# Rotary key on 128 partitions, the shifts' second half by way of DRAM, rotated queries scaled in PSUM, maxima 0.3 steps earlier

## The chip, the cores and the metric

One Trainium2 chip, one core. The metric is the device time of one execution in microseconds (us); the kernel before takes 1496.21 us, the median of 3 runs. Engines are named as in the profile: PE is TensorE (matmul), PEld its weight loads, DVE is VectorE, ACT is ScalarE, POOL is GpSimd, and SP is the queue that issues all of this kernel's DMAs. L550 is line 550 of the kernel before.

## The reference

One layer of an encoder on x of 1024 tokens by 1024 columns, all in f32. Behind the norm and one projection `h @ w_in`, two groups of eight heads attend side by side, then come an output projection and a feed-forward block with a convolution of width 3. The change touches the two groups:

```python
# group A: softmax over three dilated windows, mixed by their denominators
for window, dilation in ((128, 1), (512, 4), (2048, 16)):
    o, lse = _dilated_branch(q, k, v, slopes, window, dilation)
# group B: latent attention with one rotated key for all heads
q = (_rmsnorm(c_q, q_lat_norm) @ w_uq).reshape(b, s, N_HEADS_B, QK_NOPE + QK_ROPE)
q_rope = _rope(q[..., QK_NOPE:], cos[:, None, :], sin[:, None, :])
k_rope = _rope(k_r, cos, sin)
sc = (q_nope @ k_nope + q_rope @ k_rope) * scale
```

`_rope` turns the two halves of 32 rows: `[x1*cos - x2*sin, x2*cos + x1*sin]`.

## The kernel before

Matmuls run in pieces of a high and a low part (three matmuls for each product, L95 to L97), so TensorE has most of the work. The program is a list of events, each a function with a due time in steps (`at`, `spread`). `run` goes through it by these times; an event that is not on the main line is put behind the last main event that is `LAG` steps older. A scheduler then orders the instructions of each engine, and each engine takes them in that order, without overtaking. One step is a chunk of scores; a head of group A has eight, so head h begins at step T = 8 h.

Head h of group A needs a row of shifts before its scores: the negative maxima of its scores, so that the exponentials stay small. `a_max` spreads eight steps of maxima over T + 1.1 to T + 5.8 of the head before: L534 multiplies, L537 on VectorE adds the table and takes a maximum for each of 128 rows into `m`, 16 columns: eight for blocks in natural order, eight for blocks in the order of residues by 4. Then `a_shift` (L542) transposes `m` to 16x128 (L545), negates it on ACT into `mt`, and two DMAs (L548, L549) lay it out as two rows of 1024 on partition 96 of the head's tile, where 64 other rows are the queries and keys. One VectorE instruction on one partition, L550, reads the second row in permuted order and writes the smaller of both to partition 64. The matmuls with 65 rows (L571, L607) take this row, so the first of them waits for L550; L570 and L606, with 128 rows, don't.

Group B starts from latents: five tiles of 128 rows kept in DRAM (`latd`). `latent_pool` loads the table of cosines and sines (`rope`, 128x2x1024) and the raw rotary key to partitions 64 to 128 of `kr`. `rope_key` (L783 to L785) turns the key with three VectorE instructions on 32 partitions of 1024 elements. `key_rows` puts the result as high and low part (L791 on ACT, L792 on VectorE) into rows 64 to 96 of one head tile, and a DMA (L794) copies them to the other. `scale_queries` loads the row of the queries' norm, `rq`, to all partitions and multiplies both halves of `rope` by it on GpSimd (L756), so that `rope_steps` (L879 to L881, twice for each of two groups of four heads) only multiplies the projection by the table. For the other queries L919 scales the projection in PSUM.

The maxima of group B (L944 matmul, L945 row maximum, L950 the larger of two halves, L952 the transposition) and its V projections (`bv_steps`, into `VH` and `VL` by L212) begin while head 7 of group A still runs. L968 is its first score. `pbank` gives out the PSUM banks, `eng` the engine from the table `ENG`.

## Time and profile before

| | us |
|---|---|
| median of 3 runs (1493.6 to 1498.79) | 1496.21 |
| the profiled execution | 1493.47 |
| its span | 1491.6 |
| PE busy | 1406.6 (94%) |
| DVE busy | 975.0 (65%) |
| ACT busy | 705.4 (47%) |
| POOL busy | 532.5 (36%) |

The mean granted clock of TensorE is 0.975. All times in the rows are from the start of this one execution's span, which takes 1.9 us less than the execution itself and 4.6 us less than the median. Group A's heads run until about 435 us, group B's until about 705; the output projection and the feed-forward block come behind. The shares over the whole span say little on a stage: in 40 slices PE has nine tenths or more nearly everywhere, and 7 in two slices between 335 and 410 us.

### The profile page before, as it was taken

The page shows a single profiled execution, that of the slowest core. Times are in us where ns is not written, and L with a number is a line of the kernel's source. Part 1 is how long each engine was busy: PE and PEld are TensorE (multiplying, and loading weights), DVE is VectorE, ACT ScalarE, POOL GpSimd, SP SyncE. Part 2 cuts the span into 40 slices and gives each one's busy share as a digit, 9 for nine tenths or more (in the row PEclk, how much of TensorE's full clock was granted, in tenths as well). Part 3 has the DMA queues.
Part 4 walks back from the last instruction along what each step waited for, and adds up shares of the span by engine and source line. Part 5 has one row for each costly group of instructions (what it writes and reads, how often), then busy time and mean ns, then how long its engine had stood idle before and what let it go on. Part 6 is the DMA issues. An engine that isn't in the chain of part 4 may idle for free.

```text
span 1491.6 us, 18735 instructions
## 1 busy us (share of the span) xinstructions
PE 1406.6 (94%) x6481; PEld 1117.6 (75%) x6481; DVE 975.0 (65%) x1637; ACT 705.4 (47%) x1274; POOL 532.5 (36%) x443
## 2 busy tenths in 40 slices
PE   7999999997899999899988699999999999999998
PEld 6788887876676677566666478888888887788886
DVE  6465453438876766443588778766666675884687
ACT  6244343325455556644644454444444444454444
POOL 3132222215444543322425355555555552000110
PEclk9999999997999999999999799999999999999999
DMA  5522343556434222630125023333333323864435
GB/s 189 122 70 64 79 102 87 171 136 188 95 72 105 61 44 66 163 75 25 60 96 179 26 80 118 107 107 106 100 100 104 107 92 120 288 213 150 120 98 198
DMA packets 135903, 167.06 MB, mean 112 GB/s; under 512 B 17443, under 2 KB 93616, under 8 KB 134144
## 3 DMA queue, kind: packets, MB, share of 16 engines
q1 hardware_dynamic: 135808, 165.87, 37.8%
q8 instruction: 51, 0.84, 0.2%
q14 instruction: 44, 0.36, 0.1%
HBM read 106.12 MB, written 39.43 MB: 98 GB/s over the span
## 4 chain that ended last, share of the span: by engine, by line
PE 53%; DVE 6%; ACT 3%; POOL 3%; issue 2%; DMA 1%; SPq 0%; DVEq 0%; POOLq 0%; ACTq 0%
PE u_pu L1268 4%; PE u_pu L1266 4%; PE u_pu L1267 4%; PE v_pu1v L1266 3%; PE v_pu1v L1268 3%; PE v_pu1v L1267 3%; PE X_acc L1507 2%; PE X_acc L1508 2%; PE X_acc L1506 2%; PE Y_acc L1508 2%; PE Y_acc L1507 2%; PE Y_acc L1506 2%; PE g_pu1g L1267 2%; PE g_pu1g L1268 2%; PE g_pu1g L1266 2%
## 5 line engine op out<-in xcount | busy, mean ns | idle before, releaser
L348 POOL TENSOR_TENSOR pl_pA<-sx_pA,ph_pA 128x512 fp32r<-128x512 f32 (+1 forms) x125 | 162.7, 1307 | 263.1 <-ACT sx_pA L92 129.8
L1246 POOL TENSOR_TENSOR w_pF<-S_pF,w_pF 128x512 fp32r<-128x512 f32 x88 | 128.6, 1463 | 108.1 <-ACT w_pF L92 77.5
L1246 POOL TENSOR_TENSOR w_pF<-wf_pF,w_pF 128x512 fp32r<-128x512 f32 x66 | 89.2, 1352 | 95.7 <-ACT w_pF L92 95.3
L95 PE MATMUL proj_psx<-hT_hT,wh_pA 128*128 128x512 f32 (+2 forms) x304 | 119.6, 393 | 0.0
L97 PE MATMUL proj_psx<-hT_hT,wl_pA 128*128 128x512 f32 (+2 forms) x304 | 118.4, 389 | 0.0
L96 PE MATMUL proj_psx<-hT_hT,wh_pA 128*128 128x512 f32 (+2 forms) x304 | 118.2, 389 | 0.1
L945 DVE TENSOR_REDUCE m_pA<-mx_psy 128x1 f32<-128x512 f32 x126 | 84.1, 687 | 33.6 <-PE mx_psy L944 32.6
L92 ACT ACTIVATE w_pF<-S_pF 128x512 fp32r<-128x512 f32 x88 | 55.1, 628 | 78.6 <-PE u_pu L1268 40.1
L92 ACT ACTIVATE w_pF<-ar_pD 128x512 fp32r<-128x512 f32 x77 | 48.6, 631 | 92.4 <-PE Y_acc L1508 43.7
L92 ACT ACTIVATE sx_pA<-s_ps 128x512 f32<-128x512 f32 x128 | 75.1, 597 | 30.7 <-PE s_ps L970 17.4
L1266 PE MATMUL u_pu<-T_h2T,w_pF 128*128 128x512 f32 x220 | 86.4, 394 | 1.5 <-ACT c_h2T L92 1.5
L1267 PE MATMUL u_pu<-T_h2T,w_pF 128*128 128x512 f32 x220 | 86.4, 393 | 0.0
L1268 PE MATMUL u_pu<-T_h2T,w_pF 128*128 128x512 f32 x220 | 86.2, 392 | 0.1
L1468 DVE TENSOR_TENSOR w_pF<-ar_pD,w_pF 128x512 fp32r<-128x512 f32 x77 | 55.6, 722 | 46.8 <-ACT w_pF L92 46.7
L337 DVE TENSOR_TENSOR sx_pA<-s_ps,tab_pA 128x256 f32<-128x256 f32 (+1 forms) x128 | 48.3, 410 | 53.4 <-PE s_ps L607 34.1
L537 DVE CUSTOM_DVE_ANT_0 mx_psx<-mx_psx,tab_pA 128x256 f32<-128x256 f32 (+1 forms) x112 | 47.2, 421 | 47.9 <-PE mx_psx L534 44.5
L229 POOL TENSOR_TENSOR wl_pA<-wf_pA,wh_pA 128x256 fp32r<-128x256 f32 x48 | 37.4, 805 | 112.8 <-ACT wh_pA L92 100.1
L92 ACT ACTIVATE ph_pA<-s_ps 128x512 fp32r<-128x512 f32 x85 | 50.5, 597 | 46.7 <-PE s_ps L970 46.3
L1507 PE MATMUL X_acc<-w_pF,w_pF 128*128 128x512 f32 x176 | 68.9, 391 | 2.3 <-DVE w_pF L1470 2.3
L1506 PE MATMUL X_acc<-w_pF,w_pF 128*128 128x512 f32 x176 | 68.5, 389 | 0.0
L1508 PE MATMUL X_acc<-w_pF,w_pF 128*128 128x512 f32 x176 | 68.5, 389 | 0.0
L97 PEld LDWEIGHTS proj_psx<-hT_hT,wl_pA 128*128 128x128 f32 (+1 forms) x304 | 57.4, 189 | 12.7 <-issue 0.4
(453 smaller groups left out, 4125.9 us busy)
## 6 DMA issues: line engine op xcount, KB each, us to landing
wf_pF<-in_w_up SPq DMA_DIRECT2D x44, 512.0 KB
ar_pD<-aD_dr SPq DMA_DIRECT2D x77, 256.0 KB
head_pA<-x_xr SPq DMA_DIRECT2D x22, 512.0 KB
aD_dr<-vt_aT SPq DMA_DIRECT2D x44, 256.0 KB
B_pD<-in_w_down SPq DMA_DIRECT2D x44, 256.0 KB
aD_dr<-gt_aT SPq DMA_DIRECT2D x33, 256.0 KB
wf_pA<-in_w_in SPq DMA_DIRECT2D x16, 512.0 KB
head_pA<-x_xr SPq DMA_DIRECT2D x24, 256.0 KB
```

The source lines that it names most:

```text
L92: nc.scalar.activation(o, i, func, **kw)
L95: i = mm(ps, ah, bh, start=first, stop=False)
L96: mm(ps, ah, bl, start=False, stop=False)
L97: mm(ps, al, bh, start=False, stop=last)
L348: e.tensor_tensor(pl[:, cs], pf[:, cs], f32(ph[:, cs]), op=ALU.subtract)
L1246: nc.gpsimd.tensor_tensor(w[:, 1], src, f32(w[:, 0]), op=ALU.subtract)
L1266: mm(bank, w[:, 0, k], m[:, 0, k], start=first, stop=False, skip_group_check=True)
L1267: mm(bank, w[:, 0, k], m[:, 1, k], start=False, stop=False, skip_group_check=True)
L1268: mm(bank, w[:, 1, k], m[:, 0, k], start=False, stop=last, skip_group_check=True)
L1506: mm(bank, wa[:, 0, ts], wb[:, 0], start=first, stop=False, skip_group_check=True)
L1507: mm(bank, wa[:, 0, ts], wb[:, 1], start=False, stop=False, skip_group_check=True)
L1508: mm(bank, wa[:, 1, ts], wb[:, 0], start=False, stop=last, skip_group_check=True)
```

## The change

The shift (`a_shift`): the first eight columns go to partitions 96 to 104 of the head's tile, eight rows of 128. The other eight go to a small DRAM array `shiftd` and come back from there in permuted order, 1024 runs of one element, onto the same eight partitions. The min is then an 8x128 instruction, and a fourth DMA lays its result out as the row on partition 64. The rotary key: `kr` is now 128 partitions by four blocks of 256, loaded by four DMAs (both halves of the key, cosine, sine), turned by three VectorE instructions and split by ACT and a fourth; two DMAs store high and low part in DRAM (`krd`), and each head tile gets its rows by two loads from there. The rotated queries: L756 is gone, and the projection is scaled in PSUM by a new VectorE instruction ahead of L879. The maxima of heads 1 to 6 are due from T + 0.8 to T + 5.2.

```diff
-                a_max(h + 1, T + 1.1, T + 5.8)
+                a_max(h + 1, T + 0.8, T + 5.2)
...
-        nc.sync.dma_start(f32(ht[96:97, 2, :]), mt[0:8, :])
-        nc.sync.dma_start(f32(ht[96:97, 3, :]), mt[8:16, :])
-        eng("min", 0).tensor_tensor(ht[64:65, 2, :].rearrange("p (i r) -> p i r", r=4),
-                                f32(ht[96:97, 2, :]).rearrange("p (i r) -> p i r", r=4),
-                                f32(ht[96:97, 3, :]).rearrange("p (r i) -> p i r", r=4), op=ALU.min)
+        d = shiftd[h % 2]
+        m = ht[96:104, 2:4, :P]
+        nc.sync.dma_start(f32(m[:, 0]), mt[0:8, :])
+        nc.sync.dma_start(d, mt[8:16, :])
+        nc.sync.dma_start(f32(m[:, 1]).rearrange("i (q r) -> i q r", r=4), d.rearrange("(r j) (b q) -> (j b) q r", j=2, b=4))
+        eng("min", 0).tensor_tensor(m[:, 0], f32(m[:, 0]), f32(m[:, 1]), op=ALU.min)
+        nc.sync.dma_start(f32(ht[64:65, 2, :]), f32(m[:, 0]))
...
         nc.sync.dma_start(L["rq"], rowd[1].partition_broadcast(P))
-        for i in range(2):
-            t = L["rope"][:, i, :]
-            eng("rope", i).tensor_tensor(t, t, L["rq"], op=ALU.mult)
...
-        L["kr"] = L["p"].t([P, S], "kr")
+        L["kr"] = L["p"].t([P, 4, 256], "kr", F32R)
...
-        nc.sync.dma_start(L["kr"][64:128], latd[2, :64])
+        for i, part in enumerate((latd[2, :32], latd[2, 32:64], rope[0, 64:96], rope[1, 96:128])):
+            nc.sync.dma_start(f32(L["kr"][:, i]), part.rearrange("d (a b) -> (d a) b", a=4))
...
-        t = pa.t([P, S], "tmp", bufs=2)[0:32]
-        eng("kr", 0).tensor_tensor(t, kr[96:128], rp[96:128, 1, :], op=ALU.mult)
-        eng("kr", 1).tensor_tensor(kr[0:32], kr[64:96], rp[64:96, 0, :], op=ALU.mult)
-        eng("kr", 2).tensor_tensor(kr[0:32], kr[0:32], t, op=ALU.subtract)
+        for i in range(2):
+            nc.vector.tensor_tensor(kr[:, i], kr[:, i], kr[:, 2 + i], op=ALU.mult)
+        nc.vector.tensor_tensor(kr[:, 0], kr[:, 0], kr[:, 1], op=ALU.subtract)
+        act(split[:, 1], kr[:, 0])
+        nc.vector.tensor_tensor(split[:, 2], kr[:, 0], kr[:, 1], op=ALU.subtract)
+        for i in range(2):
+            nc.sync.dma_start(krd[i].rearrange("d (a b) -> (d a) b", a=4), kr[:, 1 + i])
...
-        if i == 0:
-            act(ht[64:96, 1, :], L["kr"][0:32])
-            eng("kr", 3).tensor_tensor(ht[64:96, 3, :], L["kr"][0:32], f32(ht[64:96, 1, :]), op=ALU.subtract)
-        else:
-            nc.sync.dma_start(f32(ht[64:96, 1::2, :]), f32(htiles[0][64:96, 1::2, :]))
+        for j in range(2):
+            nc.sync.dma_start(f32(ht[64:96, 1 + 2 * j, :]), krd[j])
...
+            nc.vector.tensor_tensor(pt, pt, L["rq"][:, cs], op=ALU.mult)
             nc.vector.tensor_tensor(t1[:, cs], pt, rp[:, 0, cs], op=ALU.mult)
```

In the changed kernel most lines stand two to six further down: L548 is there L553, L534 is L536, L537 is L539, L337 is L339, L945 is L951, L950 is L956, L220 is L222.

SP's queue around the shift of head 0, before. `mt` holds the transposed maxima, `head` is the head's tile, `wf` a tile for weights, and what stands in brackets are the counters that SP waits for before it issues (DMAHW a DMA's landing):

```order
L220 DMA wf_pA_798<-in_w_in 128x8x128 [waits DMAHW6_49,DMAHW7_49,DVE_49,Pool_49]
L548 DMA head_pA_297<-mt_pA_572 1x8x128 [waits DMAHW0_49,Activation_49]
L549 DMA head_pA_297<-mt_pA_572 1x8x128 [waits DMAHW1_49]
L220 DMA wf_pA_999<-in_w_in 128x8x128 [waits DMAHW2_49,DMAHW7_49,DVE_49,Pool_49]
L220 DMA wf_pA_1229<-in_w_in 128x8x128 [waits DMAHW2_49,DMAHW3_49,DVE_49,Pool_49]
```

The same place now:

```order
L222 DMA wf_pA_807<-in_w_in 128x8x128 [waits DMAHW6_49,DMAHW7_49,DVE_49,Pool_49]
L553 DMA head_pA_299<-mt_pA_574 8x128 [waits DMAHW0_49,Activation_49]
L554 DMA shiftd_dr_87<-mt_pA_574 8x128 [waits DMAHW1_49]
L222 DMA wf_pA_1005<-in_w_in 128x8x128 [waits DMAHW2_49,DMAHW7_49,DVE_49,Pool_49]
L555 DMA head_pA_299<-shiftd_dr_87 8x128x1 [waits DMAHW3_49,DMAHW1_49]
L557 DMA head_pA_299<-head_pA_299 1x8x128 [waits DMAHW4_49,DVE_49]
L222 DMA wf_pA_1240<-in_w_in 128x8x128 [waits DMAHW2_49,DMAHW5_49,DVE_49,Pool_49]
```

Ahead of the weight load nothing has moved, but between the store into DRAM and the gather (L555) stands the weight load that waits for GpSimd and VectorE; L557 waits for the min on VectorE.

VectorE around the rotary key, before. `kr` is the key, `mx` and `m` belong to the maxima of head 6, `sx` to the scores of head 5, `VL` to the V projection:

```order
L537 ISA m_pA_3116 128x1
L337 TENSOR_TENSOR sx_pA_3287<-s_ps_3280,tab_pA_2278 128x256
L783 TENSOR_TENSOR tmp_pA_3169<-kr_lat_3112,rope_lat_3111 32x1024
L784 TENSOR_TENSOR kr_lat_3112<-kr_lat_3112,rope_lat_3111 32x1024
L212 TENSOR_TENSOR VL_pA_3055<-proj_psx_3219,VH_pA_3054 128x256
L785 TENSOR_TENSOR kr_lat_3112<-kr_lat_3112,tmp_pA_3169 32x1024
L537 ISA mx_psx_3293,m_pA_3116<-mx_psx_3293,tab_pA_2962 128x256
L537 ISA m_pA_3116 128x1
L337 TENSOR_TENSOR sx_pA_3344<-s_ps_3337,tab_pA_2278 128x256
```

The same place now:

```order
L339 TENSOR_TENSOR sx_pA_3367<-s_ps_3360,tab_pA_2290 128x256
L788 TENSOR_TENSOR kr_lat_3132<-kr_lat_3132 128x256
L214 TENSOR_TENSOR VL_pA_3069<-proj_psx_3239,VH_pA_3068 128x256
L539 ISA mx_psx_3291,m_pA_3080<-mx_psx_3291,tab_pA_2976 128x256
L539 ISA m_pA_3080 128x1
L339 TENSOR_TENSOR sx_pA_3367<-s_ps_3360,tab_pA_2290 128x256
L539 ISA mx_psx_3318,m_pA_3080<-mx_psx_3318,tab_pA_2976 128x256
L539 ISA m_pA_3080 128x1
L788 TENSOR_TENSOR kr_lat_3132<-kr_lat_3132 128x256
L539 ISA mx_psx_3318,m_pA_3080<-mx_psx_3318,tab_pA_2976 128x256
L539 ISA m_pA_3080 128x1
L789 TENSOR_TENSOR kr_lat_3132<-kr_lat_3132 128x256
```

The three instructions that stood nearly back to back now stand apart, with maxima and additions between them.

VectorE while head 7 of group A runs, before. `sx` are its scores, L945 the row maxima of group B's first head:

```order
L945 TENSOR_REDUCE m_pA_3744<-mx_psx_3745 128x1
L337 TENSOR_TENSOR sx_pA_3738<-s_ps_3731,tab_pA_3416 128x256 x2
L945 TENSOR_REDUCE m_pA_3744<-mx_psx_3748 128x1
L337 TENSOR_TENSOR sx_pA_3777<-s_ps_3770,tab_pA_3416 128x256
L337 TENSOR_TENSOR sx_pA_3777<-s_ps_3770,tab_pA_3416 128x192
L945 TENSOR_REDUCE m_pA_3744<-mx_psy_3755 128x1
L945 TENSOR_REDUCE m_pA_3744<-mx_psy_3758 128x1
L945 TENSOR_REDUCE m_pA_3744<-mx_psy_3783 128x1
L945 TENSOR_REDUCE m_pA_3744<-mx_psy_3786 128x1
L212 TENSOR_TENSOR VL_pA_3698<-proj_psy_3789,VH_pA_3697 128x2x128
L945 TENSOR_REDUCE m_pA_3744<-mx_psy_3806 128x1
```

The same stretch of head 7's additions now:

```order
L339 TENSOR_TENSOR sx_pA_3801<-s_ps_3794,tab_pA_3436 128x256
L339 TENSOR_TENSOR sx_pA_3801<-s_ps_3794,tab_pA_3436 128x192
L339 TENSOR_TENSOR sx_pA_3856<-s_ps_3849,tab_pA_3436 128x256 x2
L339 TENSOR_TENSOR sx_pA_3889<-s_ps_3882,tab_pA_3436 128x256 x2
L339 TENSOR_TENSOR sx_pA_3929<-s_ps_3922,tab_pA_3436 128x256 x2
L339 TENSOR_TENSOR sx_pA_3952<-s_ps_3945,tab_pA_3436 128x256 x2
L634 TENSOR_TENSOR y_xr_103<-pv_ps_3915,y_xr_103 65x2x256
L345 CAST ph_pA_3950<-sx_pA_3952 128x512
L951 TENSOR_REDUCE m_pA_3768<-mx_psx_3769 128x1
L350 TENSOR_TENSOR pl_pA_3951<-sx_pA_3952,ph_pA_3950 128x512
L951 TENSOR_REDUCE m_pA_3768<-mx_psx_3772 128x1
L634 TENSOR_TENSOR y_xr_103<-pv_ps_3961,y_xr_103 65x2x256
```

The row maxima and the V parts that stood between the additions now begin behind the last addition of head 7.

## Rows read from the trace of the kernel before

**Rows 1.** Windows: us, then busy us (instructions) of five engines, granted clock, DMA share, GB/s.

```profile
60.00:336.00 276.00, 270.89 (x1380) 222.21 (x1381) 137.79 (x398) 101.83 (x214) 71.14 (x77) 0.98 0.38 99
336.00:373.00 37.00, 27.51 (x150) 24.12 (x149) 31.47 (x77) 19.18 (x36) 22.29 (x13) 0.77 0.60 185
373.00:410.00 37.00, 31.13 (x170) 25.58 (x168) 33.11 (x52) 17.28 (x35) 16.16 (x16) 0.91 0.42 96
```

**Rows 2.** Windows of four us, same columns.

```profile
362.00:366.00 4.00, 0.29 (x1) 0.29 (x2) 4.00 (x9) 0.03 (x1) 4.00 (x2) 0.50 0.66 144
366.00:370.00 4.00, 3.30 (x14) 2.79 (x14) 3.00 (x9) 3.21 (x6) 2.19 (x3) 0.50 0.42 140
```

**Rows 3.** Waits of PE, 336 to 425 us: who <- for whom: us, times, longest.

```profile
PE mx_psx L534 <- DVE m_pA L537: 7.6, 2, 4.4
PE pv_ps L591 <- DVE ph_pA L343: 1.8, 1, 1.8
PE s_ps L571 <- DVE head_pA L550: 1.6, 1, 1.6
```

**Rows 4.** Waits of PE, 60 to 336 us.

```profile
PE s_ps L571 <- DVE head_pA L550: 1.2, 2, 0.8
```

**Rows 5.** Timeline of DVE: start us, us, engine, line, operation, out<-in, shapes.

```profile
345.32 2.30 DVE L192 SCALAR_TENSOR_TENSOR ls_pA<-nt_const,ls_pA 128x8 f32<-128x8 f32 x1
...
356.85 2.77 DVE L783 TENSOR_TENSOR tmp_pA<-kr_lat,rope_lat 32x1024 f32<-32x1024 f32 x1
359.63 2.20 DVE L784 TENSOR_TENSOR kr_lat<-kr_lat,rope_lat 32x1024 f32<-32x1024 f32 x1
...
362.21 2.37 DVE L785 TENSOR_TENSOR kr_lat<-kr_lat,tmp_pA 32x1024 f32<-32x1024 f32 x1
...
379.85 3.51 DVE L550 TENSOR_TENSOR head_pA<-head_pA 1x1024 fp32r<-1x1024 f32 x1
...
393.58 1.92 DVE L550 TENSOR_TENSOR head_pA<-head_pA 1x1024 fp32r<-1x1024 f32 x1
...
395.53 0.39 DVE L343 CAST ph_pA<-sx_pA 128x448 fp32r<-128x448 f32 x1
...
401.32 1.22 DVE L792 TENSOR_TENSOR head_pA<-kr_lat,head_pA 32x1024 fp32r<-32x1024 f32 x1
```

**Rows 6.** Timeline of POOL.

```profile
344.67 2.92 POOL L778 TENSOR_TENSOR cq_lat<-x_xr,cq_lat 128x1024 fp32r<-128x1024 f32 x1 [0.85 <-ACT cq_lat L92]
...
376.82 4.77 POOL L756 TENSOR_TENSOR rope_lat<-rope_lat,rq_lat 128x1024 f32<-128x1024 f32 x2
```

**Rows 7.** Single lines: ns min/median/max, first and last start, forms.

```profile
L229 DVE TENSOR_TENSOR wl_pA<-wf_pA,wh_pA x16: 362/426/1295, 10.9 to 310.1; 128x256 fp32r<-128x256 f32 x16
L950 DVE TENSOR_TENSOR m_pA<-m_pA x10: 129/162/1275, 418.3 to 702.4; 128x8 f32<-128x8 f32 x6, 128x4 f32<-128x4 f32 x4
L919 DVE TENSOR_TENSOR proj_psx<-proj_psx,rq_lat x2: 689/694/700, 376.7 to 383.4; 128x512 f32<-128x512 f32 x2
```

**Rows 8.** Timeline of PE, head 0; in brackets idle time before, and its releaser.

```profile
68.42 0.27 PE L545 MATMUL mx_psx<-ident_const,m_pA 128*16 128x128 f32 x1
...
76.46 0.36 PE L571 MATMUL s_ps<-head_pA 65*128 65x192 f32 x1 [0.79 <-DVE head_pA L550]
```

**Rows 9.** Timeline of SP, ACT and DVE: copies and who used them.

```profile
69.02 0.74 SPq L548 DMA_DIRECT2D head_pA<-mt_pA  x1
...
182.66 0.37 SPq L727 DMA_DIRECT2D wf_pA<-in_w_in  x1
...
185.42 0.51 ACT L92 ACTIVATE wf_pA<-wf_pA 128x128 f32<-128x128 f32 x2 [1.70 <-DMA wf_pA<-in_w_in]
...
240.67 0.67 SPq L549 DMA_DIRECT2D head_pA<-mt_pA  x1
...
242.76 2.04 DVE L550 TENSOR_TENSOR head_pA<-head_pA 1x1024 fp32r<-1x1024 f32 x1
```

**Rows 10.** Window of the handover, columns as in rows 1.

```profile
403.00:425.00 22.00, 19.93 (x126) 16.81 (x125) 18.98 (x40) 12.45 (x25) 8.98 (x8) 1.00 0.30 58
```

More of the change, by code (lines that the diff above doesn't have):

```diff
@@ L114, in layer_kernel @@
     PH, PL, SX = 4, 4, 2
-    ENG = {"scale": ["p", "v"], "ckv": ["v", "p"], "cq": ["v", "p", "p"], "rope": ["p", "p"], "qr": ["v", "p"],
+    ENG = {"scale": ["p", "v"], "ckv": ["v", "p"], "cq": ["v", "p", "p"], "qr": ["v", "p"],
            "sq": ["v", "p", "v", "p"], "rows": ["v", "p", "p", "p", "v", "v", "p", "v"], "wl": ["v", "p", "p", "p"],
-           "min": ["v"], "fin": ["v", "v", "v", "v"], "kr": ["v", "v", "v", "v"]}
+           "min": ["v"], "fin": ["v", "v", "v", "v"]}
     def eng(name, i):
@@ L173, in layer_kernel @@
     yraw = dr.t([4, P, S], "yraw")
+    shiftd = dr.t([2, 8, P], "shiftd")
+    krd = dr.t([2, 32, S], "krd")
     yd2 = dr.t([2, P, S], "yd2")
@@ L764, in latent_pool @@
         L["rope"] = L["p"].t([P, 2, S], "rope")
-        L["kr"] = L["p"].t([P, S], "kr")
+        L["kr"] = L["p"].t([P, 4, 256], "kr", F32R)
         L["rq"] = L["p"].t([P, S], "rq")
-        nc.sync.dma_start(L["rope"], rope)
-        nc.sync.dma_start(L["kr"][64:128], latd[2, :64])
+        nc.sync.dma_start(L["rope"], rope.rearrange("i p t -> p i t"))
+        for i, part in enumerate((latd[2, :32], latd[2, 32:64], rope[0, 64:96], rope[1, 96:128])):
+            nc.sync.dma_start(f32(L["kr"][:, i]), part.rearrange("d (a b) -> (d a) b", a=4))
     def split_keys(k):
@@ L780, in rope_key @@
     def rope_key():
-        rp, kr = L["rope"], L["kr"]
-        t = pa.t([P, S], "tmp", bufs=2)[0:32]
-        eng("kr", 0).tensor_tensor(t, kr[96:128], rp[96:128, 1, :], op=ALU.mult)
-        eng("kr", 1).tensor_tensor(kr[0:32], kr[64:96], rp[64:96, 0, :], op=ALU.mult)
-        eng("kr", 2).tensor_tensor(kr[0:32], kr[0:32], t, op=ALU.subtract)
+        split = L["kr"]
+        kr = f32(split)
+        for i in range(2):
[5 more added lines that the diff above has]
+            nc.sync.dma_start(krd[i].rearrange("d (a b) -> (d a) b", a=4), kr[:, 1 + i])
     def key_rows(i):
@@ L1621, in _consts @@
     sin = np.tile(np.sin(ang).astype(np.float32).T, (4, 1))
-    rope = np.stack([np.tile(cos, (8, 1)), np.concatenate([sin, -sin], 0)], 1)
+    rope = np.stack([np.tile(cos, (8, 1)), np.concatenate([sin, -sin], 0)], 0)
     slope = 2.0 ** -np.arange(1, HA + 1)[:, None, None]
```

## The prediction

> **What bounds the kernel now.** First I read the busy time by stage [rows 1]. From 60 to 336 us TensorE is busy 270.89 of 276 us and VectorE only half: there a VectorE instruction counts only where TensorE stands waiting for it. From 336 to 410 us, the last two heads of group A with the latents of group B, it is the other way round: TensorE is busy 27.51 of 37 us and 31.13 of 37, at a granted clock of 0.77 and 0.91, while VectorE has 31.47 and 33.11. From 403 on TensorE leads again, 19.93 of 22 us [rows 10]. Then the bad stage in steps of four us [rows 2]: from 362 to 366 VectorE fills 4.00 of 4.00 and TensorE has 0.29. Then TensorE's waits there [rows 3]: 7.6 us in two waits for L537's maxima, 1.8 for the cast L343, 1.6 for the shift's min L550. VectorE's own order of time [rows 5] names what stood ahead of each. L783 to L785, the rotary key on 32 partitions (2.77, 2.20 and 2.37 us), run until 364.6, and the longest wait for L537, 4.4 us, lies over them; L550 at 379.85 took 3.51 us and held the first scores of head 6; L550 at 393.58 (1.92 us) stood ahead of the cast L343 at 395.53. The change shortens just these, so its worth is decided between 336 and 425 us, by VectorE's sum there.
>
> **Rotary key.** Gone: 2.77 + 2.20 + 2.37 = 7.34 us, and L792's 1.22 [rows 5]. New: four instructions of 128x256. The nearest row is L229 on VectorE, same size, both inputs in SBUF: 0.36 to 1.30 us, median 0.43 [rows 7]. At the median that is 1.7 us and the saving 5.6. But instructions with both inputs in SBUF are slow here when GpSimd works: L192, a 128x8 one, took 2.30 us from 345.32 to 347.62, and GpSimd's L778 ran from 344.67 to 347.59 [rows 5, 6]. So the small instruction stood until GpSimd's big one was done. GpSimd is busy 22.29 of 37 us in this stage [rows 1], 60%, with instructions up to 2.92 us [rows 6]; an instruction that meets one in 6 of 10 cases and then waits half of some 2.0 us loses 0.6 us, which I add to each, and the four cost 4 x 1.03 = 4.1. Saving 3.2 us, between 5.6 and, at 1.83 each (0.43 and half of 2.8 for every one), nothing. The Trainium skill has this as a rule (SBUF — State Buffer, "Who interferes with whom"): a VectorE instruction with two SBUF inputs and a GpSimd one that reads SBUF exclude each other, and the later one waits for the whole of the earlier. The L192 row agrees to 0.03 us. The rule speaks against the change, since four short instructions can meet GpSimd four times where three long ones met it three times. With L792, this part gives -4.4 us of VectorE. The SP queue gets five small loads and stores more; the store L793 waits for VectorE and stands ahead of the load of the queries' scale. The key's last rows are wanted only by group B, after 400 us, so I take nothing for it.
>
> **The shifts' min.** Each L550 goes (2.0 us in the first six heads, 3.51 and 1.92 in the last two) and an 8x128 min comes. Nearest is L950, 128x8: 0.13 to 1.28 us, median 0.16 [rows 7]; with the same 0.6 for GpSimd, 0.8. Heads 6 and 7: -5.4 + 1.6 = -3.8 us, between -5.1 and, at 2.3 each like L192, -0.8. In the first six heads VectorE has room, and only heads 0 and 1 made TensorE wait, 1.2 us in all [rows 4]. The new way is longer on SP: two copies out, one gather from DRAM of 1024 runs of four bytes, the min, a copy into row 64. Its length from the transposition: 0.60 us until the first copy is issued (68.42 to 69.02), 0.74 for that issue [rows 8, 9], at most 2.1 for a 4 KB copy from issue to use (240.67 to 242.76), then the gather. The nearest row for that is L727, 1024 runs of 128 bytes, used 2.76 us after its issue (182.66 to 185.42) [rows 9]; then 0.8 and again 2.1. Sum 9.1 us. TensorE's cover: head 0's transposition and its first shifted score lay 8.04 us apart, 0.79 of that waiting [rows 8]. The order of the changed kernel puts 1.5 times as many columns between them (head 0; 1.4 times at head 1, 1.2 at head 4, 1.6 at head 6), since the maxima start earlier; 7.25 x 1.5 is 10.9 us. The chain fits by about 1.8 us and the 1.2 us of waiting go; I take half, -0.6, because SP issues in order and a weight load that waits for GpSimd stands between the store and the gather at heads 0, 3 and 4. The Trainium skill (DMA: Bandwidth & Descriptors, "Rules for kernel authors") says that a strided last dimension becomes one descriptor per element, and names a fixed cost of about 2.0 us per transfer. As an estimate from that page, three transfers in a row are 6 us before the gather's 1024 elements cost anything, and the chain 8.1 us instead of 9.1 plus what they cost. No run here shows a gather of four-byte runs.
>
> **Rotated queries.** The two GpSimd instructions L756 go, 4.77 us at 376.82 [rows 6]. This frees L550 at 379.85, which is gone anyway. Four scalings in PSUM come, 0.69 us each like L919 [rows 7]: two in the bad stage, +1.4, hidden in no way since VectorE is the bound there, and two in group B, where TensorE leads from the start [rows 10]: nothing, or +0.3 if they land on a wait.
>
> **Maxima 0.3 steps earlier.** The same instructions move; TensorE is full there. It provides the cover used above. Nothing by itself, within 1 us either way.
>
> **Sum.** VectorE between 336 and 425 us: -4.4 - 3.8 + 1.4 = -6.8, bounds -10.4 and about +1. TensorE waited 4.4 + 1.6 + 1.8 = 7.8 us behind these very instructions [rows 3, 5], but not all of it comes back: GpSimd's share of the work is next, 60% busy there [rows 1], and so are the other waits on its results. I take three quarters, -5.1. The granted clock adds: over the wait of 4.4 us and the four us behind it, it was 0.50 [rows 2], the lower level of 1.2 GHz, so 3.30 us of TensorE's work there would take 1.65 at 2.4 GHz; half of what that gives back, -0.7. With -0.6 from heads 0 and 1 the sum is -6.4 us. The profiled execution took 1493.47 us, so 1487.1 on its base. It lies 2.7 us below the median of the runs, 1496.21; on the median's base it is **1489.8 us**.
>
> **Rivals.** (A) *The handover to group B eats the gain.* In the order of the changed kernel head 7's scores come without the maxima of group B's first head and without the V projections that filled TensorE between them; both come in a block behind them. From 403 to 425 us VectorE was busy 18.98 of 22 [rows 10]. Now head 7 is bound by its additions, and then TensorE by nine row maxima of 0.69 us (6.2 us) before the first score of group B can go. For it: TensorE has nothing else there. Against it: VectorE's sum is what it was, and V projections lie beside the maxima. Price: the 2.1 us of TensorE's idle time doubles, and a fall of the clock as in [rows 2] adds 2: about +4, giving 1494. (B) *GpSimd takes the saving back.* If each of the four key instructions and both mins wait for half of a GpSimd instruction of 2.8 us, the VectorE sum is -1.2 + 0 - 5.4 + 3.1 + 1.4 = -2.1, and with the rest -3: 1493. This is how it would go if the rule of the Trainium skill (SBUF — State Buffer, "Who interferes with whom") hit every time. (C) *The chain comes late, and the kernel is slower.* This starts when the gather takes over 4.6 us (2.76 plus the 1.8 spare). Then heads 0, 1, 4 and 6, with the shortest cover, wait. At 7.5 us each loses 2.9 and about 0.6 by the clock, 14 us, against a gain of 5.8 elsewhere: +8, 1504. At 6 us: 4 x 1.7 less 5.8 = +1, no change. For it: 1024 runs of four bytes appear nowhere in the trace, and VectorE is blocked in order behind a min that waits. Against it: L727 has as many runs. (D) *All of the saving shows*, with no meeting on GpSimd: -10.4 - 1.5 - 1.2, 1483.
>
> **Chances.** The forecast's case, -3.5 to -9: 0.45. D: 0.08. A and B, alone or together, between -3.5 and +4: 0.30. C: 0.17. About 0.3% (4.5 us) is what a measurement of this kernel can tell from no change. Of the forecast's case about one part in six lies inside that. Faster 0.46, within 0.36, slower 0.18. The range leaves out D's far end and the far part of C: 1481 to 1502; the forecast's own case is 1487 to 1493.
>
> **What would show it.** Right: L783 to L785's successors at 0.4 to 1.1 us; no TensorE wait over 2 us between 355 and 385; the granted clock of 336 to 373 up from 0.77 to 0.85 or more; first score of group B some 5 us earlier. Wrong: a wait of TensorE for the row of shifts at heads 0, 1, 4 or 6 (C); a stage 403 to 425 with TensorE under 85% (A); the new instructions over 1.2 us each (B). If the gather's landing is over 5 us the forecast is wrong in its sign.

## The result, and the profile after

The changed kernel takes 1514.66 us, the median of 4 runs (1511.34 to 1519.48), against 1496.14 us for the kernel before in 4 runs: a ratio of 1.012, 95% interval 1.0097 to 1.0143. It is 18.5 us slower. The forecast was 1489.8 us, a gain of 6.4, and the range ended at 1502. The profiled execution of after took 1516.91 us, with a span of 1515.0 us and a mean granted clock of 0.966; that of before is 23.4 us shorter.

The first section of the page of after, by engine: busy us, share of the span, instructions.

```profile
PE 1422.4 (94%) x6481; PEld 1126.2 (74%) x6481; DVE 959.0 (63%) x1641; ACT 705.6 (47%) x1274; POOL 522.2 (34%) x441
```

Before, VectorE had 975.0 us and GpSimd 532.5. So the change did take work away, 16.0 us of VectorE's and 10.3 of GpSimd's, and the kernel became slower. TensorE does the same 6481 matmuls, and its busy time grew by 15.8 us, at a mean granted clock of 0.966 in place of 0.975; the other 7.6 us by which the profiled execution is longer are idle time of TensorE. Now the stages that [rows 1] showed, with the one behind them. Busy time of each engine in a stretch, then the granted clock, the DMA share and GB/s; after:

```profile
60.00:336.00 276.00, 269.15 (x1355) 220.16 (x1355) 125.83 (x392) 101.03 (x214) 69.04 (x78) 0.97 0.38 98
336.00:373.00 37.00, 30.89 (x162) 26.64 (x162) 26.84 (x80) 17.14 (x37) 15.12 (x13) 0.83 0.52 176
373.00:410.00 37.00, 27.68 (x122) 21.83 (x122) 24.95 (x40) 13.07 (x22) 11.16 (x10) 0.80 0.41 92
410.00:448.00 38.00, 32.14 (x176) 26.40 (x176) 26.53 (x53) 16.56 (x31) 12.31 (x12) 0.87 0.40 84
```

The last stretch before:

```profile
410.00:448.00 38.00, 36.16 (x192) 28.07 (x193) 29.28 (x55) 20.99 (x44) 18.68 (x19) 1.00 0.34 74
```

The stage the prediction aimed at, 336 to 373 us, did get better: TensorE is busy 30.89 us in place of 27.51, at a granted clock of 0.83 in place of 0.77, and VectorE has 4.6 us less [rows 1]. But 373 to 410 fell from 31.13 us at 0.91 to 27.68 at 0.80, and 410 to 448 from 36.16 at the upper level (2.4 GHz) to 32.14 at 0.87.

These windows are fixed in time, and the changed kernel runs some us late in them. To follow where the time goes, one more reading: all matmuls of a trace in order of time, the columns they pass summed up; the **lag** at t is how much later than t the other kernel has passed as many columns as before had at t. All these kernels pass the same sum. The lag in us, by the time of before (single executions: those of the kernel before lie between 1489.7 and 1503.6, so a lag of two or three us says nothing; the one read here is 2.7 us below its median, that of the shift alone, 1501.12 us, is the fastest of its ten):

```
t                  96    224    328    368    376    392    408    432    456    480    end
after            +1.6   +6.1   +7.4   +1.2   +7.6  +13.2  +10.4  +19.4  +23.2  +18.7  +23.5
shift alone      +2.8   +2.8   +3.1   -0.3   +2.7  +11.6   +9.6   +9.6   +9.6   +8.1   +7.7
key alone        +0.9   +0.9   +2.4   -4.1   +3.5   +3.9   +2.2  +12.8  +17.7  +13.2  +16.3
queries alone    +0.3   +0.3   +0.2   +0.3   +1.2   -0.5   +0.4   +4.0   +4.0   +4.0   +6.0
maxima alone     -0.6   +3.0   +6.5   +4.4   +7.5   +9.8   +9.2   +9.3   +9.3   +7.9   +8.8
without shift    +0.8   +2.7   +6.7   +2.1   +9.0   +7.8   +9.4  +16.4  +20.5  +16.1  +18.1
```

After is 7 us late by 328 us, makes 6 good up to 368, loses them again within 8 us and 5.6 more by 392, and loses another 9 between 408 and 432. Behind 480 another 4.8 are added. Of the 7 us by 328 only 1.6 are there at 96 us, behind the start of head 0. The changed kernel without its shift has 6.7 there, and the maxima alone have 6.5: in these traces that loss goes with the maxima more than with the shift. The kernels of the single rows stand in the section on the experiments.

**Head 0.** In the changed kernel, SP, VectorE and TensorE around the first shift (start, duration, instruction, idle time before it and what ended it):

```profile
69.68 0.45 SPq L554 DMA_DIRECT2D shiftd_dr<-mt_pA  x1
71.95 0.39 SPq L222 DMA_DIRECT2D wf_pA<-in_w_in  x1
72.44 0.76 SPq L555 DMA_DIRECT2D head_pA<-shiftd_dr  x1
78.17 0.67 SPq L557 DMA_DIRECT2D head_pA<-head_pA  x1
...
77.86 0.29 DVE L556 TENSOR_TENSOR head_pA<-head_pA 8x128 fp32r<-8x128 f32 x1 [2.00 <-DMA head_pA<-shiftd_dr]
...
79.29 0.84 PE L536 MATMUL mx_psx<-head_pA 128*128 128x256 f32 x2 [0.93 <-DVE m_pA L539]
...
80.66 0.25 PE L576 MATMUL s_ps<-head_pA 65*128 65x192 f32 x1
```

The gather (L555) stands behind the weight load L222, which waits until 71.95, and 5.42 us lie between the gather's issue and the min. VectorE stands still for 2.00 us of them, and the maxima of the next head (L539), queued behind the min, are what TensorE then waits for, 0.93 us. The first shifted score comes at 80.66, before at 76.46 [rows 8].

**The key's successors** were priced well in their sum, and TensorE's wait of 4.4 us behind the old key [rows 3] is gone. The groups of L788, L789 and L791 (durations min, median, max in ns, then first and last start):

```profile
L788 DVE TENSOR_TENSOR kr_lat<-kr_lat x2: 419/1358/2298, 364.9 to 369.2; 128x256 f32<-128x256 f32 x2
L789 DVE TENSOR_TENSOR kr_lat<-kr_lat x1: 1335/1335/1335, 369.9 to 369.9; 128x256 f32<-128x256 f32 x1
L791 DVE TENSOR_TENSOR kr_lat<-kr_lat x1: 415/415/415, 371.8 to 371.8; 128x256 fp32r<-128x256 f32 x1
```

**Head 6.** TensorE's waits of 336 to 410 us, after (us in total, times, longest), in place of [rows 3]:

```profile
PE s_ps L575 <- DVE sx_pA L339: 3.5, 1, 3.5
PE s_ps L611 <- DVE sx_pA L339: 2.6, 1, 2.6
PE pv_ps L628 <- POOL pl_pA L350: 2.5, 1, 2.5
PE mx_psx L536 <- DVE m_pA L539: 2.4, 4, 0.7
```

The 7.6 us for the maxima are 2.4 now, and up to 425 us as well, but new waits stand beside them. The longest, for L339, is at 398.05: VectorE had the six instructions of the rotated queries (L884 at 392.35 to L894 until 397.3) ahead of head 6's first additions.

### The profile page after: what moved, and what is told of

Same layout as the page of the kernel before. It is cut to its first block, busy times and chain, and to the rows that moved or that the text cites. A ratio compares the mean times of both kernels' runs of the same rounds, so it can differ in the third digit from the quotient of the medians.

```text
span 1515.0 us, 18777 instructions
## 1 busy us (share of the span) xinstructions
PE 1422.4 (94%) x6481; PEld 1126.2 (74%) x6481; DVE 959.0 (63%) x1641; ACT 705.6 (47%) x1274; POOL 522.2 (34%) x441
## 4 chain that ended last, share of the span: by engine, by line
PE 70%; DVE 10%; ACT 5%; POOL 4%; issue 3%; DMA 3%; SPq 1%; DVEq 0%; POOLq 0%; ACTq 0%
PE u_pu L1272 4%; PE u_pu L1273 4%; PE u_pu L1274 4%; PE proj_psx L95 3%; PE proj_psx L97 3%; PE proj_psx L96 3%; PE v_pu1v L1272 3%; PE v_pu1v L1274 3%; PE v_pu1v L1273 3%; PE X_acc L1513 2%; PE X_acc L1514 2%; PE X_acc L1512 2%; PE Y_acc L1514 2%; PE Y_acc L1513 2%; PE Y_acc L1512 2%
## 5 line engine op out<-in xcount | busy, mean ns | idle before, releaser
L350 POOL TENSOR_TENSOR pl_pA<-sx_pA,ph_pA 128x512 fp32r<-128x512 f32 (+1 forms) x125 | 161.2, 1293 | 287.9 <-ACT sx_pA L92 197.8
L951 DVE TENSOR_REDUCE m_pA<-mx_psy 128x1 f32<-128x512 f32 x126 | 83.9, 685 | 31.2 <-PE mx_psy L950 30.5
L339 DVE TENSOR_TENSOR sx_pA<-s_ps,tab_pA 128x256 f32<-128x256 f32 (+1 forms) x128 | 48.2, 410 | 52.4 <-PE s_ps L612 37.4
L539 DVE CUSTOM_DVE_ANT_0 mx_psx<-mx_psx,tab_pA 128x256 f32<-128x256 f32 (+1 forms) x112 | 47.1, 421 | 54.1 <-PE mx_psx L536 51.6
```

The lines of the kernel that those rows point to most:

```text
L350: e.tensor_tensor(pl[:, cs], pf[:, cs], f32(ph[:, cs]), op=ALU.subtract)
```

## The experiments

Ratios are to the kernel before on the same chip, with 95% intervals. Each kernel below is the kernel before with the edit named, unless it says otherwise.

**Each part alone.** Four kernels, each with one part of the diff of the change and nothing of the others: the shift, the key, the queries, the maxima. The key's part holds a line of the diff that the cut ahead of the prediction leaves out: the table of cosines and sines lies in DRAM as two blocks of 128x1024, so that the key's rows of each can be loaded by themselves. The cores of the edits:

```diff
only_shift
+        nc.sync.dma_start(d, mt[8:16, :])
...
+        nc.sync.dma_start(f32(ht[64:65, 2, :]), f32(m[:, 0]))
only_key
+        L["kr"] = L["p"].t([P, 4, 256], "kr", F32R)
...
+            nc.sync.dma_start(f32(ht[64:96, 1 + 2 * j, :]), krd[j])
only_rope
-            eng("rope", i).tensor_tensor(t, t, L["rq"], op=ALU.mult)
...
+            nc.vector.tensor_tensor(pt, pt, L["rq"][:, cs], op=ALU.mult)
only_max
-                a_max(h + 1, T + 1.1, T + 5.8)
+                a_max(h + 1, T + 0.8, T + 5.2)
```

> The kernel before with the new shift alone (four transfers, 8x128 min); maxima, key and rotated queries as before. Theory: the new shift carries the loss. It brings 1024 runs of four bytes that land 4.2 to 5.7 us after their issue in the changed kernel, VectorE stands in order behind the min, and the maxima don't start earlier to cover it: +12 to +22 us, 1508 to 1518. Rival, the loss comes from the order of the work around the last two heads, which the key and the rotated queries have moved: within +4 us, under 1500.

> The kernel before with the rotary key on 128 partitions alone. Theory: it takes 4.4 us off VectorE in the stage that VectorE bounds: -2 to -4 us, 1492 to 1494. Rival, the store and the loads on SP and the scheduler's new order at head 6 cost what it saves and more: +3 to +10 us.

> The kernel before with the rotated queries scaled in PSUM alone: GpSimd loses 4.8 us, VectorE gains four instructions of 0.7 us. Theory: the min of head 6 is no longer held by GpSimd (3.51 to 2.0 us) and two scalings are added: -1 to +1 us, no change. Rival, the order behind it moves and head 7 loses its filling: +4 to +10 us.

> The kernel before with the maxima due 0.3 steps earlier alone. Theory: the same work in the stage that TensorE bounds, no change, within 2 us. Rival, VectorE takes the earlier maxima ahead of the additions that TensorE's chunks wait for, and heads 1 to 5 lose the 5 us that the changed kernel lost by 330 us: +4 to +7 us.

Measured: shift 1.0070 (1.0047 to 1.0094), key 1.0087 (1.0056 to 1.0118), queries 1.0028 (1.0011 to 1.0044), maxima 1.0055 (1.0039 to 1.0070). Every part makes the kernel slower by itself, and the four sum to 2.40% where all together cost 1.20%. No part is the one culprit. The maxima stand out: no instruction is added, removed or changed, and the kernel loses 0.55%.

**The change without its shift**, to see whether the other three keep a gain that the shift eats. After with the old `a_shift`:

```diff
-        nc.sync.dma_start(d, mt[8:16, :])
...
+        eng("min", 0).tensor_tensor(ht[64:65, 2, :].rearrange("p (i r) -> p i r", r=4),
```

> The changed kernel with the old shift (two copies, the min on one partition); key, rotated queries and earlier maxima stay. Alone, the parts cost 9.6 (shift), 13.3 (key), 4.2 (queries) and 6.7 us (maxima), 33.8 in sum, and all together 18.3. Theory: the shift's cost stands by itself, so +8 to +10 us are left, 1505. Rival: the parts cost the same idle time at the last two heads, and the time follows the key alone: +14 to +20 us, 1511 to 1516.

Measured 1.0082 (1.0054 to 1.0111). They keep none. By the two numbers the shift is about a third of the loss, and it is not what turns the sign.

**The key's rows earlier.** In only_key the two loads of each head tile's key rows stand on SP behind the stores of head 6's output. SP of only_key, then of key_early, in which only the due times of `key_rows` are moved:

```profile
412.57 0.49 SPq L632 DMA_DIRECT2D yraw_dr<-y_xr  x1
413.11 0.43 SPq L633 DMA_DIRECT2D dend_dr<-y_xr  x1
413.60 1.05 SPq L798 DMA_DIRECT2D head_pA<-krd_dr  x2
```

```profile
403.15 0.99 SPq L798 DMA_DIRECT2D head_pA<-krd_dr  x2
404.23 0.53 SPq L936 DMA_DIRECT2D head_pA<-x_xr  x1
```

```diff
-    at(57.87, lambda: key_rows(0))
-    at(65.98, lambda: key_rows(1))
+    at(56.5, lambda: key_rows(0))
+    at(64.2, lambda: key_rows(1))
```

> The kernel with the key alone on 128 partitions, with the two events that load the key's rows into the head tiles moved ahead of the rest of the tiles' assembly (due 56.5 and 64.2 instead of 57.87 and 65.98). Theory: the key's 13.3 us come from these loads, which stand on SP behind the store of head 6's result, so that the maxima of group B's first head start late: -2 to +4 us against before, 1494 to 1500. Rival: the cost lies in the turning itself (four short VectorE instructions, DRAM), between 340 and 380 us: still +9 to +14.

> The changed kernel with the key's row loads ahead of the assembly, as in the kernel with the key alone. Theory: it wins back the handover's part, some 9 us between 410 and 460 us: +7 to +11 us against before, 1503 to 1507. Rival, the maxima of group B are late for the same reason as head 7 (all is late by the shift): no gain, +16 to +19.

Measured: key_early 1.0028 (1.0013 to 1.0042), where only_key has 1.0087: 9 us come back by two numbers. after_early, the same edit on after: 1.0079 (1.0050 to 1.0108) against 1.012, 6 us, though these two intervals overlap. The first maximum of group B, a matmul of 96 rows, shows how. In order: before, only_key, key_early, after.

```profile
408.86 0.39 PE L944 MATMUL mx_psx<-head_pA 96*128 96x512 f32 x1
```

```profile
427.46 0.63 PE L948 MATMUL mx_psx<-head_pA 96*128 96x512 f32 x1
```

```profile
416.16 0.42 PE L948 MATMUL mx_psx<-head_pA 96*128 96x512 f32 x1
```

```profile
434.48 0.63 PE L950 MATMUL mx_psx<-head_pA 96*128 96x512 f32 x1
```

Before, group B's maxima stood between the scores of head 7 from 409 us on and filled TensorE's gaps there. With the rows loaded late, head 7's scores go without that filling, and the maxima come in a block behind them. From 408 to 424 and 424 to 440 us (busy time by engine, then the clock), before and only_key:

```profile
408.00:424.00 16.00, 14.97 (x93) 12.68 (x94) 14.26 (x30) 9.93 (x20) 6.72 (x7) 1.00 0.12 26
424.00:440.00 16.00, 16.00 (x86) 12.67 (x85) 11.84 (x21) 9.15 (x19) 7.77 (x8) 1.00 0.54 114
```

```profile
408.00:424.00 16.00, 13.31 (x84) 11.88 (x82) 8.49 (x20) 10.77 (x20) 7.88 (x8) 0.89 0.42 90
424.00:440.00 16.00, 12.78 (x52) 8.90 (x52) 12.27 (x22) 2.44 (x7) 1.89 (x3) 0.79 0.29 60
```

The trace of only_key has 136 matmuls there where that of before has 179. TensorE's idle time is 5.9 us where it was 1.0, and the clock falls from 1.00 to 0.89 and 0.79. TensorE does not wait for the rows themselves: the first maximum starts 12.8 us after the second load has been issued in only_key and 12.0 us after it in key_early, and no wait for these loads stands in TensorE's timeline. So the two due times work by the order that the scheduler makes from them; what the place on SP costs by itself isn't shown.

**The gather's runs of four bytes.** shift_flat is only_shift with the gather reading eight runs of 512 bytes. It leaves out the permutation of the second half, so its row of shifts is another.

```diff
-        nc.sync.dma_start(f32(m[:, 1]).rearrange("i (q r) -> i q r", r=4), d.rearrange("(r j) (b q) -> (j b) q r", j=2, b=4))
+        nc.sync.dma_start(f32(m[:, 1]), d)
```

> The kernel with the new shift alone, the gather read in the order in which it lies, eight runs of 512 bytes instead of 1024 of four. It leaves out the permutation, so its shifts are a mix of wrong rows; its work is the same. Theory: the gather's 4.2 to 5.7 us are what VectorE stands behind, and it falls to about 2: +3 to +5 us against before instead of +9.6. Rival: four transfers in a row, or the order, cost it: +8 to +11.

Measured 1.0057 (1.0041 to 1.0074), only_shift 1.0070. Head 4's gather and min, only_shift and then shift_flat:

```profile
245.26 0.73 SPq L554 DMA_DIRECT2D head_pA<-shiftd_dr  x1
249.56 0.29 DVE L555 TENSOR_TENSOR head_pA<-head_pA 8x128 fp32r<-8x128 f32 x1 [4.07 <-DMA head_pA<-shiftd_dr]
```

```profile
246.32 0.26 SPq L554 DMA_DIRECT2D head_pA<-shiftd_dr  x1
247.80 0.29 DVE L555 TENSOR_TENSOR head_pA<-head_pA 8x128 fp32r<-8x128 f32 x1 [1.31 <-DMA head_pA<-shiftd_dr]
```

From issue to use the gather goes from 4.30 us to 1.48, and VectorE's waits for it, over all heads, from 12.2 us to 1.6. The time gains 2 us by the two ratios, inside the intervals. My theory that the short runs make the loss falls; most of VectorE's waiting cost nothing at the end.

**Which heads carry it.** The new shift in heads 6 and 7 only, 0 to 5, 0 alone, 1 to 5; the others keep the old one:

```diff
+        if h < 6:
+            d = shiftd[h % 2]
...
+        else:
+            nc.sync.dma_start(f32(ht[96:97, 2, :]), mt[0:8, :])
```

> The new shift for heads 6 and 7 alone, the old one for heads 0 to 5. In all heads it costs 9.6 us. Theory: two thirds of it arise at head 6, where the last copy is issued at 389.8 us and head 6's chunks come some 6 us late: +5 to +7 us. Rival: heads 0 to 5 carry it, and what is late at head 6 is late already: within +3.

> The new shift for heads 0 to 5 alone. Theory: a third of the 9.6 us, at heads 0 and 3, where VectorE stands up to 2 us behind the gather: +2 to +4 us. Rival: +6 to +10.

> The new shift for head 0 alone, the old one for all others. Theory: at head 0 the weight load between the store and the gather puts the row of shifts 2.4 us later, TensorE idles some 1.2 us more, and its granted clock falls (0.68 and 0.50 in 80 to 88 us where it was 1.00): +2.5 to +4 us. Rival: what is lost there comes back before 336 us: within +1.

> The new shift for heads 1 to 5 alone. Theory: the rest of the 9 us of heads 0 to 5, at head 3 and at the stage from 336 us, which all this reaches later and in another order: +4 to +7 us. Rival: head 0 carries nearly all: within +2.

Measured: heads 6 and 7 0.9999 (0.9987 to 1.0011), heads 0 to 5 1.0068 (1.0044 to 1.0092), head 0 1.0013 (0.9995 to 1.0031), heads 1 to 5 1.0029 (1.0013 to 1.0046). The loss of only_shift is in heads 0 to 5; where I counted a gain, in 6 and 7, there is none. Single traces don't agree on where it surfaces: only_shift has 8.9 of its lag between 376 and 392 us, shift_05 has 6.9 of 11.6 by 224. How heads 0 to 5 share it isn't resolved either: the two parts sum to 0.42% and the whole has 0.68%, with intervals that overlap. Head 0 in shift_05, then before, from 76 us:

```profile
76.00:80.00 4.00, 2.77 (x12) 2.03 (x12) 1.23 (x5) 0.00 (x0) 0.00 (x0) 1.00 0.06 2
80.00:84.00 4.00, 3.73 (x19) 2.97 (x18) 3.30 (x10) 3.29 (x7) 1.98 (x3) 0.68 0.01 1
84.00:88.00 4.00, 4.00 (x17) 3.49 (x16) 1.99 (x6) 1.54 (x3) 1.40 (x2) 0.50 0.47 131
```

```profile
76.00:80.00 4.00, 3.54 (x22) 3.20 (x23) 3.77 (x12) 1.85 (x3) 0.00 (x0) 1.00 0.00 0
80.00:84.00 4.00, 4.00 (x27) 3.47 (x26) 3.02 (x11) 2.90 (x6) 2.05 (x2) 1.00 0.00 0
84.00:88.00 4.00, 4.00 (x23) 3.32 (x22) 3.03 (x10) 1.40 (x5) 2.67 (x4) 1.00 0.03 6
```

In shift_05 TensorE was idle 1.23 us, and behind that the clock stood at 0.68 and then 0.50, the lower level (1.2 GHz). In the same 12 us the profiled execution of after kept 1.00 and had 2.0 us of idle time, so the clock's part isn't the same in each run.

**Rotated queries out of the way of head 6.** only_shift showed its lag at 392 us, where in after the rotation stood ahead of head 6's additions. only_shift with `rope_steps(0)` later:

```diff
-    spread(rope_steps(0), 49.74, 54.26)
+    spread(rope_steps(0), 51.5, 56.0)
```

> The kernel with the new shift alone, and the rotated queries of group B's first heads due 1.75 steps later (51.5 to 56.0 instead of 49.74 to 54.26), so that head 6's first additions stand ahead of the six rotation instructions on VectorE. Theory: the part of the shift's loss at head 6 (some 6 us of 9.6) comes from the rotation, 4.2 us long, in front of these additions: +3 to +6 us against before. Rival: the row of shifts itself is late (389.8 us issue of the last copy, 6 us later than the old min ended), and the order behind it does not matter: +8 to +11.

Measured 1.0082 (1.0056 to 1.0108), no better than only_shift. In its trace the rotation did move behind head 6's first additions. These start at 395.72 all the same (only_shift 395.63), behind 1.54 us in which VectorE waits for TensorE's scores; by its lag this trace is 4 us later than that of only_shift already at 376 us. This theory falls, and with heads 6 and 7 alone costing nothing there is no loss left for it to explain.

**The maxima the other way.** If the move of 0.3 steps costs because earlier is worse, later should be better; if any move costs, it should be slower too.

```diff
-                a_max(h + 1, T + 1.1, T + 5.8)
+                a_max(h + 1, T + 1.4, T + 6.4)
```

> The kernel before with the maxima due 0.3 steps later and more spread (T + 1.4 to T + 6.4), against 0.3 earlier, which alone cost 6.7 us. No instruction is added or removed. Theory: the times of before are a tuned point, and any move of the order costs: +3 to +10 us. Rival: earlier maxima are bad by themselves (VectorE and SP take them ahead of what a chunk waits for), and later ones are no worse than before: within 2 us or faster.

Measured 1.0031 (1.0014 to 1.0048). Both directions lose, 0.55% and 0.31%, with the same instructions; in both the start moves by 0.3 steps and the end by 0.6. What moves is the order alone, in which the scheduler fits matmuls, maxima and weight work into each other. Of the three settings that of before is the best. That its other due times fit its durations as closely, so that any change of a duration loses something, would explain why all four parts lose; these runs support it and don't prove it.

**What takes the key's gain.** By its lag key_early is 4.2 us early at 368 us and 3.3 late at 376. The same 16 us of before and key_early:

```profile
360.00:368.00 8.00, 2.66 (x11) 1.77 (x9) 7.65 (x16) 1.25 (x3) 6.80 (x3) 0.56 0.62 155
368.00:376.00 8.00, 7.00 (x32) 5.12 (x32) 6.83 (x11) 5.31 (x14) 7.38 (x7) 0.80 0.01 3
```

```profile
360.00:368.00 8.00, 7.13 (x34) 5.80 (x32) 7.23 (x24) 4.78 (x10) 4.61 (x5) 0.84 0.32 103
368.00:376.00 8.00, 4.39 (x14) 2.73 (x13) 7.97 (x6) 3.24 (x9) 5.82 (x4) 0.50 0.60 153
```

The hole behind the old key is filled, and the same hole opens 8 us later. What ends it is the projection of the latents, at 374.00, which waited 2.39 us for ACT's split `ckv`, and that for the scaling of the latents by the norm's row (L750, before L749). The load of that row had moved: SP of before and of key_early.

```profile
354.48 0.34 SPq L746 DMA_DIRECT2D tmp_pA<-rowd_dr  x1
```

```profile
363.77 0.82 SPq L792 DMA_DIRECT2D krd_dr<-kr_lat  x2
364.68 0.40 SPq L747 DMA_DIRECT2D tmp_pA<-rowd_dr  x1
```

The store L792 waits 9.8 us for ACT's high part of the key that VectorE turned, and holds back the load L747 by 10 us. I took this load for the cause. But the scaling on GpSimd did not wait for it: it starts 5.4 us after the load's issue, straight behind the weights' split. GpSimd in key_early:

```profile
367.59 2.51 POOL L822 TENSOR_TENSOR wl_pA<-wf_pA,wh_pA 128x768 fp32r<-128x768 f32 x1
370.07 2.79 POOL L750 TENSOR_TENSOR x_xr<-x_xr,tmp_pA 128x1024 f32<-128x1024 f32 x1
```

Two edits on top of key_early, one on top of the other: key_store gives the two stores a later event of their own, and key_scale, with that, moves to VectorE the one of the two scalings that GpSimd has. before_scale does the latter on before, and after_early_store does the former on after_early.

```diff
+    def rope_key_out():
+        kr = f32(L["kr"])
...
+    at(50.0, rope_key_out)
...
-    ENG = {"scale": ["p", "v"], "ckv": ["v", "p"], "cq": ["v", "p", "p"], "rope": ["p", "p"], "qr": ["v", "p"],
+    ENG = {"scale": ["v", "v"], "ckv": ["v", "p"], "cq": ["v", "p", "p"], "rope": ["p", "p"], "qr": ["v", "p"],
```

> The kernel with the key alone and its row loads ahead of the assembly (1500.2), and the two stores of the turned key due at 50.0 instead of right behind the turning, so that they stand on SP behind the load of the keys' norm row and not ahead of it. Theory: in the kernel without this the norm row was issued at 364.7 us, behind the store that waits for VectorE, instead of 354.5, and TensorE got back 6.4 us by 368 and lost 7.5 by 376; now the gain stays: -2 to -7 us against before, 1488 to 1493. Rival: the scaling and splitting of the keys are late by VectorE's own order: still +2 to +5.

> The changed kernel with both moves of the key's transfers (row loads ahead of the assembly, stores behind the norm row). With the first alone it took 1508.7. Theory: the same 4 to 8 us as in the kernel with the key alone: 1501 to 1505. Rival: head 6's transposition is late by other causes (the shift, the maxima), and the key's stores hide behind it: 1507 to 1511.

> The kernel with the key alone and both moves of its transfers (1503.2), and both scalings of the keys' latents on VectorE instead of one on GpSimd. In the kernel without this the stall at the key's turning is gone (5.7 us ahead of before by 368 us), but GpSimd takes two other instructions ahead of the weights' split and the scaling, the keys' latents are split 3.5 us later than before, and TensorE waits 2.8 us for them. Theory: it is this order of GpSimd that takes the gain back, and with the scaling off GpSimd 3 to 6 us of it stay: 1496 to 1500. Rival: something later takes it anyway (the shift's min at head 6, the queries): 1502 to 1505.

> The kernel before with both scalings of the keys' latents on VectorE, nothing else: the control for the last one. Theory: VectorE bounds that stage, so 1.2 us more on it costs 0 to +5 us. Rival: GpSimd's scaling was what TensorE waited for already: -2 to -5 us.

Measured: key_store 1.0054 (1.0038 to 1.0070), after_early_store 1.0081 (1.0054 to 1.0108), key_scale 1.0025 (1.0007 to 1.0044), before_scale 1.0019 (1.0009 to 1.0028). The load moved as meant, to 352.04 in key_store, and the kernel gained nothing, since GpSimd's order stayed what it was in key_early. GpSimd in before, then in key_store:

```profile
360.72 2.78 POOL L818 TENSOR_TENSOR wl_pA<-wf_pA,wh_pA 128x768 fp32r<-128x768 f32 x1
363.46 3.34 POOL L749 TENSOR_TENSOR x_xr<-x_xr,tmp_pA 128x1024 f32<-128x1024 f32 x1
```

```profile
366.11 3.63 POOL L826 TENSOR_TENSOR wl_pA<-wf_pA,wh_pA 128x768 fp32r<-128x768 f32 x1
369.71 2.79 POOL L750 TENSOR_TENSOR x_xr<-x_xr,tmp_pA 128x1024 f32<-128x1024 f32 x1
```

The weights' split and the scaling start 5 to 6 us later than before, behind two more instructions L349 of the running head; in before the two stand behind the scaling (L348, from 368.62). The projection starts at 373.63, before at 371.56. With the scaling on VectorE it comes at 370.69, but at 374.47 TensorE waits again, 2.81 us, for the split on GpSimd:

```profile
374.47 0.80 PE L97 MATMUL proj_psx<-cq_lat,wl_pA 128*128 128x512 f32 x1 [2.81 <-POOL wl_pA L826]
```

So behind the key's hole lay another, of GpSimd's chain for the latents: without its scaling the split of the weights is last. Why the scheduler put the two L349 ahead isn't shown. No version of these beats the kernel before. What the key kernels with early rows lose behind 480 us (key_early has +2.6 at 480 and +6.8 at 560, after_early +7.5 at 480 and +15.1 at the end) I haven't explained.

## Why the prediction was wrong

The step that failed is the one from VectorE's sum between 336 and 425 us to the end of the kernel. The sum itself was right: the key's instructions took 4.1 us less, the mins of heads 6 and 7 took 0.29 and 0.96 us in place of 3.51 and 1.92, and two scalings added 1.4: -6.9 us, where I had -6.8. I took three quarters of it, -5.1, as coming to the end, and nothing came. The key with early rows is 4 us slower than before (1.0028), and the new shift in heads 6 and 7 alone changes nothing (0.9999). Beside that, the terms that I put at nothing or close to it (the key's last rows, heads 0 to 5, the maxima, the queries' place) are where the kernel loses. Point by point:

- **The key's instructions**: right in their sum. I put four at 4.1 us; they took 0.42, 2.30, 1.34 and 0.42, or 4.5. The longest two lie outside the 0.4 to 1.1 us that I named. They follow the pattern of L192 [rows 5, 6]: each ends 0.27 or 0.28 us behind a GpSimd instruction that began before it (L782 until 366.91, L350 until 370.93). The wait they were to remove is gone, and the clock of 336 to 373 us rose from 0.77 to 0.83, short of the 0.85 that I named. My other signs of being right failed: TensorE waits 2.53 us at 377.58 for GpSimd's L350, and the first score of group B comes at 447.9 us, before at 424.6. What I had wrong is what comes next. I put GpSimd's share and the other waits at a quarter of the gain, and in the key kernels they took all of it: the lag of the key alone is -4.1 at 368 and +3.5 at 376 us, and it is GpSimd's chain for the latents that holds TensorE there.
- **The key's last rows**: "wanted only by group B, after 400 us, so I take nothing for it". This term is 9 us by key_early against only_key. I had counted five more DMAs on SP, and even named rival A's block of maxima, but didn't ask what the rows' due times do to the order of the maxima. Rival A, the handover, was priced at +4 for the doubled idle time and a fall of the clock; from 408 to 432 us after loses 9.0. The sign that I named for it, TensorE under 85% from 403 to 425, did not show (19.41 of 22 us, 88%, at 0.96); the hole lies behind, from 410 to 448 us, with 32.14 of 38 us, 85%, at 0.87.
- **The shifts' min**: the 8x128 min took 0.29 us in most heads, less than the 0.8 that I took. But the gain in heads 6 and 7, my -3.8, is nothing (0.9999), and heads 0 to 5, which I put at -0.6, cost about 10 us (1.0068). This is the largest single miss. I had a gather of 2.76 us in the chain of 9.1; in heads 0 to 5 of after it took 4.2 to 5.7. So rival C's condition (over 4.6 us) was met at heads 0, 4 and 5 in that trace, and so was my sign for a wrong forecast, a landing over 5 us. But its mechanism is not what cost the time. TensorE hardly waited for the row itself (0.9 us at head 6; at head 0 it waited 0.93 us for the maxima behind the blocked min), and shift_flat, with a gather of 1.48 us, still costs 0.57%. That C's sign and size came near is luck. What else in the new chain costs heads 0 to 5 their time isn't settled. Of the weight loads ahead of the gather, which I named for heads 0, 3 and 4, the trace shows a wait at head 0 alone: the gather is issued 2.8 us behind the store there, and 1.4 us at heads 3 and 4, as at heads 1 and 2, which have no weight load there.
- **Rotated queries**: +1.4 in the sum, 4 us measured (1.0028). In the trace of only_rope the lag grows between 408 and 432 us, where none of the four scalings stands (they start at 387.44, 396.59, 519.75 and 528.97). TensorE is idle 3.2 us from 400 to 408, before 1.0, and from 408 to 424 its clock stands at 0.57 and 0.79 where before has 1.00. I had no term for that.
- **The maxima**: "Nothing by itself, within 1 us either way": +8 us (1.0055). And I had counted on their move for the cover of the longer chain. In a stage where TensorE is full at 98% [rows 1], the order of filling work counts, and it has no row of its own in the profile of before.
- **The chances**: I gave the sign that came 0.18, nearly all of it to rival C, whose mechanism the runs don't bear out. Of the rivals A came true, at about twice its price; the losses by the maxima and the queries stood in none. Their prices don't add up either: 2.40% one by one, 1.20% together.
- **The working**: two slips that decide nothing. Half of the 1.65 us that the clock was to give back is 0.8, not 0.7, and the upper bound of VectorE's sum, "about +1", is -0.6 by its own terms (-1.2, -0.8 and +1.4).

## What to carry to other kernels

Where TensorE is nearly full and the order of the work is set by due times, busy time taken off another engine is not a gain until the next late link is known. Follow the chain of the next product of that stage, queue by queue, before counting any of it, and ask of each link whether it waited or only stood behind another. Every transfer that a change adds has a due time of its own, and the order of what needs it moves with that; 9 us hung on two due times here. And try the moved due times alone and in both directions: a move without any work in it can cost as much as the work.
